# Gate and up products as seven Strassen products of halves, with the weight sums made by adding transfers

## The chip, the cores and the metric

The kernel runs on one core of one Trainium2 chip. The metric is the device time of one execution in microseconds (us). The engines are TensorE (PE, matrix products), VectorE (DVE), ScalarE (ACT), GpSimd (POOL) and SyncE (SP, which here only issues transfers); ACT and POOL issue transfers too, in order with their arithmetic. The 16 DMA engines are shared by all of them.

## The reference

One block on x of 512 rows and 1024 columns, all in float32:

```
proj  = rmsnorm(x) @ w_in
out_a = gated_delta_rule(conv(q, k, v), g, beta) -> norm, gate z -> @ w_o
out_b = silu(layernorm(conv31(glu))) @ w_pw2 + b
x  = x + (gate_a * out_a + gate_b * out_b) @ w_out
h2 = rmsnorm(x)
x  = x + (silu(h2 @ w_gate) * (h2 @ w_up)) @ w_down     # hidden width 2816
return rmsnorm(x) * norm_f_w
```

## The kernel before

A float32 product is made of three: weight and operand are each split into a high part in the matmul's format (`whi`, `hh`) and the rest (`wlo`, `hl`), and `split3` (L107 to L113) issues high x high, high x low and low x high. `unit` (L92 to L105) brings weights in: SP loads 128 x 1024 values into `raw`, ACT copies the high part (L102), DVE subtracts (L104). Each of the three has three buffers, so SP can run three units ahead.

The stages follow one another on PE: the input projection with the deltanet heads worked in between (to about 440 us), the gates, the eight column tiles of `wo` (490 to 532), the eight of `wpw` (532 to 575), `w_out` (`tok_mm`, to 621), then the channel mixer. In the wo stage the layernorm of the convolution branch is worked beside the products: ACT squares (L574), POOL sums them (L575), a root (L582), eight silu (L586), and then eight `yh` (L728) with their rests `yl` (L729), which are the operands of wpw. Behind `w_out` comes the second norm: squares on ACT (L794), POOL's `rms_half` (L796, L798), a scaling, transposes on PE and the split into `hh`, `hl` (L828).

The hidden width is 22 tiles of 128. For each tile f the gate and the up product have 8 k-tiles x 3 matmuls of 128 x 512; silu on ACT (L881), the product on DVE (L888). For f below 11 POOL also makes the sums of the down weights (`sums`, L860 to L868): one load, four additions, one store to `wsum` in DRAM. The down product is Winograd's form of Strassen: seven products of halves over 11 k-tiles, two at a time by `two`, the last one (p3) alone, with the final norm (`norm_f`, L911 to L922) running into the end.

The order on each engine is the order in which the scheduler puts the program's lines, by when their inputs come. `behind` and `issue_after` hold an instruction behind another one of its engine.

## Time and profile before

| what | value |
|---|---|
| median of 3 runs | 987.75 us (987.21 to 988.66) |
| profiled execution | 987.57 us |
| its span | 985.8 us |
| mean granted clock of PE | 0.994 |
| bytes moved by DMA | 138.50 MB |

The difference of 1.8 us between the profiled execution and its span lies around the program. In a row of a timeline the first number is the start and the second the duration in us; the bracket holds the idle time ahead of it and what ended it. In a row of a group, the number behind x is the count, then busy time and the mean of one in ns.

### The profile page before, as it was taken

Reading aid. Unit: us, or ns where it says so; the run is one execution under the profiler, and the core shown is the slowest. Engines: PE = TensorE matmul, PEld = TensorE weight load, DVE = VectorE, ACT = ScalarE, POOL = GpSimd, SP = SyncE. Lnnn points to the kernel's source line nnn. Section 1 sums busy time; section 2 is a strip of 40 time slices with the busy share of each in tenths; the row PEclk is TensorE's granted clock in tenths of the full one; section 3 lists DMA queues with packets and bytes.
Section 4 is the critical chain, followed back from the end, with each engine's and each line's share of the span. In section 5 each row is a group of like instructions: output and inputs, shape, how many; then the busy total and the mean of one; then the engine's idle time right before and its main releaser. Section 6 shows DMA issues by size and latency. Waiting matters only on the chain.

```text
span 985.8 us, 13439 instructions
## 1 busy us (share of the span) xinstructions
PE 955.7 (97%) x4775; PEld 785.7 (80%) x4775; DVE 669.8 (68%) x1044; ACT 513.6 (52%) x1062; POOL 255.1 (26%) x410
## 2 busy tenths in 40 slices
...
GB/s 317 88 119 120 120 91 41 127 68 98 77 65 88 65 87 69 97 124 144 272 137 137 146 115 65 166 192 246 186 242 206 203 211 184 92 168 196 160 207 86
DMA packets 48291, 138.50 MB, mean 140 GB/s; under 512 B 7472, under 2 KB 9424, under 8 KB 45408
## 3 DMA queue, kind: packets, MB, share of 16 engines
q1 hardware_dynamic: 44016, 112.36, 34.4%
q0 software_dynamic: 3488, 24.17, 6.9%
q10 hardware_dynamic: 720, 1.11, 0.3%
q8 instruction: 37, 0.61, 0.3%
...
## 4 chain that ended last, share of the span: by engine, by line
PE 84%; ACT 5%; DVE 4%; POOL 4%; issue 2%; DMA 1%; SPq 0%; POOLq 0%; ACTq 0%; DVEq 0%
PE mm L113 64%; PE w L113 11%; DVE wlo L104 1%; POOL Un L350 1%; ACT cp L355 1%; ACT Un L349 1%; PE st L477 1%; PE b L415 1%; PE b L421 1%; PE st L483 1%; POOL ytm L376 1%; PE st L489 1%; PE g L346 1%; DMA raw<-in_win_dram 1%; PE st L478 1%
## 5 line engine op out<-in xcount | busy, mean ns | idle before, releaser
L102 ACT ACTIVATE whi<-raw 128x1024 fp32r<-128x1024 f32 x167 | 176.1, 1057 | 327.1 <-PE mm L113 191.9
L113 PE MATMUL mm<-hh,whi 128*128 128x512 f32 x816 | 325.9, 400 | 0.0
L113 PE MATMUL mm<-hl,whi 128*128 128x512 f32 x816 | 321.9, 395 | 2.3 <-POOL hl L229 1.6
L113 PE MATMUL mm<-hh,wlo 128*128 128x512 f32 x816 | 322.3, 395 | 0.0
L104 DVE TENSOR_TENSOR wlo<-raw,whi 128x1024 fp32r<-128x1024 f32 x167 | 214.5, 1285 | 114.7 <-ACT whi L102 114.1
L545 DVE SCALAR_TENSOR_TENSOR cps<-c,c31w,cps 128x512 f32<-128x512 f32 x240 | 180.0, 750 | 4.9 <-ACT cps L543 1.0
L113 PEld LDWEIGHTS mm<-hl,whi 128*128 128x128 f32 x816 | 153.5, 188 | 33.0 <-POOL hl L229 2.9
L113 PEld LDWEIGHTS mm<-hh,wlo 128*128 128x128 f32 x816 | 153.4, 188 | 30.1
L113 PEld LDWEIGHTS mm<-hh,whi 128*128 128x128 f32 x816 | 153.5, 188 | 29.2 <-ACT hh L228 0.2
L888 DVE TENSOR_TENSOR fm<-mm,fsg 128x512 f32<-128x512 f32 x21 | 14.5, 692 | 67.0 <-PE mm L113 67.0
L300 DVE SCALAR_TENSOR_TENSOR acc<-mm,c4w,acc 128x509 f32<-128x509 f32 (+2 forms) x72 | 52.6, 738 | 1.5 <-ACT acc L297 1.2
L376 POOL TENSOR_TENSOR ytm<-U,y 128x60 f32<-128x60 f32 (+14 forms) x120 | 36.9, 307 | 60.6 <-DMA U<-sc 51.9
L113 PE MATMUL mm<-yh,whi 128*128 128x512 f32 x128 | 50.6, 396 | 0.0
L113 PE MATMUL mm<-yh,wlo 128*128 128x512 f32 x128 | 49.8, 389 | 0.0
L113 PE MATMUL mm<-yl,whi 128*128 128x512 f32 x128 | 49.8, 389 | 0.0
L113 PE MATMUL w<-whi,fh 128*128 128x512 f32 (+1 forms) x115 | 45.3, 395 | 2.8 <-ACT whi L102 2.8
L113 PE MATMUL w<-wlo,fh 128*128 128x512 f32 (+1 forms) x115 | 45.6, 397 | 2.4 <-DVE wlo L104 2.4
L113 PE MATMUL w<-whi,fl 128*128 128x512 f32 (+1 forms) x115 | 45.0, 393 | 0.0
L378 POOL TENSOR_TENSOR y<-y,ytm 128x60 f32<-128x60 f32 (+14 forms) x120 | 34.9, 291 | 9.4
L511 POOL TENSOR_TENSOR ss<-ss,half 128x4 f32<-128x4 f32 x8 | 8.1, 1014 | 109.5 <-DVE ss L509 109.5
L796 POOL TENSOR_SCALAR ss<-ss 128x1 f32<-128x1 f32 x17 | 5.7, 338 | 117.9 <-ACT sg L794 105.3
L864 POOL TENSOR_TENSOR wst<-wst 128x512 f32<-128x512 f32 x11 | 15.2, 1386 | 62.7 <-DMA wst<-in_wdn_dram 62.7
...
## 6 DMA issues: line engine op xcount, KB each, us to landing
raw<-in_win_dram SPq DMA_DIRECT2D x61, 512.0 KB, 3.3
raw<-in_wgu_dram SPq DMA_DIRECT2D x44, 512.0 KB, 3.4
...
A<-in_x_dram SPq DMA_DIRECT2D x8, 512.0 KB, 6.3
...
```

The lines of the kernel that those rows point to most:

```text
L102: marked(S.activation(hi[:, 0:n], raw[:, 0:n], AF.Copy), "unit")
L104: marked(V.tensor_tensor(out=lo[:, 0:n], in0=raw[:, 0:n], in1=hi[:, 0:n].bitcast(F32), op=ALU.subtract), "unit")
L113: marked(PE.matmul(ps, l, r, start=first and i == 0, stop=last and i == 2))
L300: marked(V.scalar_tensor_tensor(out=acc[:, s:], in0=ps[:, :T - s], scalar=c4w[:, j, k:k + 1], in1=acc[:, s:], op0=ALU.mult, op1=ALU.add))
L346: PE.matmul(ps[:, n, :], kT[:, n, :], kT[:, n, :], start=True, stop=True)
L349: S.activation(Un[:, n, :], ps[:, n, :], AF.Copy, scale=nb2[:, n:n + 1])
L350: G.tensor_tensor(out=Un, in0=Un, in1=DT, op=ALU.mult)
L376: G.tensor_tensor(out=tm[:, :, 0:w], in0=U[:, k, :, k + 1:], in1=y[:, :, k:k + 1].broadcast_to([P, NT, w]), op=ALU.mult)
L378: last[0] = G.tensor_tensor(out=y[:, :, k + 1:], in0=y[:, :, k + 1:], in1=tm[:, :, 0:w], op=ALU.add)
L545: V.scalar_tensor_tensor(out=acc, in0=c[:, k:k + T], scalar=c31w[:, i, k:k + 1], in1=acc, op0=ALU.mult, op1=ALU.add)
L864: G.tensor_tensor(out=b11, in0=b12, in1=b11, op=ALU.subtract)
L888: V.tensor_tensor(out=fm, in0=pu, in1=sg, op=ALU.mult)
```

## The change

The gate and up products of f = 2 to 21 are made together by `pair`: rows of a tile's weights (k 0 to 3, k 4 to 7) and columns of the operand (256 tokens each) are halved, and seven products of 4 k-tiles x 3 matmuls of 256 columns take the place of eight such blocks. f = 0 and 1 stay as they were. The operands' sums (`xb`, `T2`, `T3`, `T4`) are made once, on DVE and POOL. The weights' sums s1 to s4 (20 tiles of 128 x 512, 5.24 MB each) and those of the down product t1 to t4 (11 tiles, 2.88 MB each) are made in DRAM: `begin` copies one array (from ACT, four pieces), `plus` adds another to it by an accumulating transfer (from POOL, four pieces). POOL's `sums` goes. The gated values `fm` of all 22 tiles stay on chip, y1 goes to DRAM (`ysp`) after the second norm and comes back as `y2` in the first down product, and the final norm's lines are put in another order.

```diff
-    def unit(ap):
-        n = 1024
-        raw = wp.tile([P, 1024], F32, name="raw")
-        if isinstance(ap, tuple):
-            n = T * len(ap)
-            for i, p in enumerate(ap):
-                nc.sync.dma_start(raw[:, i * T:(i + 1) * T], p)
-        else:
-            nc.sync.dma_start(raw.rearrange("p (a c) -> p a c", a=2) if len(ap.shape) == 3 else raw, ap)
-        hi = wp.tile([P, 1024], F32R, name="whi")
-        marked(S.activation(hi[:, 0:n], raw[:, 0:n], AF.Copy), "unit")
-        lo = wp.tile([P, 1024], F32R, name="wlo")
-        marked(V.tensor_tensor(out=lo[:, 0:n], in0=raw[:, 0:n], in1=hi[:, 0:n].bitcast(F32), op=ALU.subtract), "unit")
+    loads = []
+    def unit(ap, pool=None):
+        aps = ap if isinstance(ap, tuple) else (ap,)
+        n = T * len(aps) if isinstance(ap, tuple) else 1024
+        raw, hi, lo = ((pool or wp).tile([P, n if pool else 1024], t, name=x)[:, 0:n]
+                       for t, x in ((F32, "raw"), (F32R, "whi"), (F32R, "wlo")))
+        for i, p in enumerate(aps):
+            loads.append(nc.sync.dma_start(raw[:, i * T:(i + 1) * T] if len(aps) > 1 else raw, p))
+        marked(S.activation(hi, raw, AF.Copy), "unit")
+        marked(V.tensor_tensor(out=lo, in0=raw, in1=hi.bitcast(F32), op=ALU.subtract), "unit")
         return hi, lo
...
+    FK, F0 = FF // 2, 2
+    sums = {n: dram.tile([FF - F0, P, T], F32, name=n, bufs=1) for n in ("s1", "s2", "s3", "s4")}
+    sums.update({n: dram.tile([FK, P, T], F32, name=n, bufs=1) for n in ("t1", "t2", "t3", "t4")})
+    gu = {n: a["wgu"][r * FF + F0:(r + 1) * FF][:, :, c * T:(c + 1) * T]
+          for n, r, c in (("A11", 0, 0), ("A12", 0, 1), ("A21", 1, 0), ("A22", 1, 1))}
+    gu.update({n: a["wdn"][:, :, c * T:(c + 1) * T] for n, c in (("B11", 0), ("B12", 1), ("B21", 2), ("B22", 3))})
+    src = lambda n: sums[n] if n in sums else gu[n]
+    def pieces(n):
+        f = sums[n].shape[0]
+        return [slice(i * f // 4, (i + 1) * f // 4) for i in range(4)]
+    def begin(n, m, ps=range(4)):
+        with behind(mybir.EngineType.Activation):
+            for p in ps:
+                nc.scalar.dma_start(sums[n][pieces(n)[p]], src(m)[pieces(n)[p]])
+    def plus(n, m, ps=range(4), behind_=None):
+        with tc.issue_after(behind_.ins) if behind_ else nullcontext():
+            for p in ps:
+                nc.gpsimd.dma_start(sums[n][pieces(n)[p]], src(m)[pieces(n)[p]], accum_op=ALU.add)
...
-                G.tensor_tensor(out=vacc, in0=vacc, in1=sq2, op=ALU.add)
+                last[0] = G.tensor_tensor(out=vacc, in0=vacc, in1=sq2, op=ALU.add)
...
+    plan = [(at + 15 * i, f, n, m, [i]) for at, f, n, m in ((100, begin, "s1", "A21"), (160, begin, "s3", "A11"))
+            for i in range(4)]
+    plan += [(at + 40 * i, f, n, m, [2 * i, 2 * i + 1]) for at, f, n, m in
+             ((165, plus, "s1", "A22"), (240, plus, "s3", "A21"), (260, begin, "s2", "s1"), (330, plus, "s2", "A11"))
+             for i in range(2)]
+    plan.sort(key=lambda p: p[0])
     while step() or chains:
+        while plan and plan[0][0] <= count[0]:
+            _, f, *w = plan.pop(0)
+            f(*w, *([last[0]] if f is plus else []))
...
         col_tile(ps, a["wo"][j], oh, ol)
+        if j == 3:
+            begin("s4", "s2")
+        if j in (5, 7):
+            begin(*(("t1", "B11") if j == 5 else ("t3", "B22")))
         ma = mp.tile([P, T], F32, name="ma", bufs=KD + 1)
...
+        if j in (0, 3, 5):
+            plus(*(("s4", "A12") if j == 0 else ("t1", "B12") if j == 3 else ("t3", "B12")), behind_=last[0])
...
         if hf:
+            nc.scalar.dma_start(ysp[n], y1[:, n, :])
...
-    def sums(k):
-        r = fp.tile([P, 4, T], F32, name="wst", bufs=1)
-        nc.gpsimd.dma_start(r, a["wdn"][k].rearrange("p (i c) -> p i c", i=4))
-        b11, b12, b21, b22 = (r[:, i, :] for i in range(4))
-        G.tensor_tensor(out=b11, in0=b12, in1=b11, op=ALU.subtract)
-        G.tensor_tensor(out=b12, in0=b22, in1=b12, op=ALU.subtract)
-        G.tensor_tensor(out=b22, in0=b22, in1=b11, op=ALU.subtract)
-        G.tensor_tensor(out=b21, in0=b22, in1=b21, op=ALU.subtract)
-        nc.gpsimd.dma_start(wsum[k], r)
...
-        if f < FK:
-            sums(f)
-            set1.append(xset())
-            hi, lo = (t[:, t1] for t in set1[f])
-            xsplit(hi, lo, fm[:, t1])
...
+    def operands(f):
+        if f < FK:
+            set1.append(xset())
+            hi, lo = (t[:, t1] for t in set1[f])
+            xsplit(hi, lo, fms[f][:, t1])
+            return
+        b, fm = fms[f - FK], fms[f]
+        s1 = fq.tile([P, TH], F32, name="s1")
+        tt(s1, b[:, t2], fm[:, t2], ALU.subtract)
+        hi, lo = (t[:, t2] for t in set1[f - FK])
+        xsplit(hi, lo, s1)
+        tt(b[:, t2], b[:, t1], b[:, t2], ALU.subtract, G)
+        last[0] = tt(b[:, t1], s1, b[:, t1], ALU.subtract, G)
...
+    kl, kh = slice(0, KH), slice(KH, KD)
+    xb = []
+    for i, (ks, ts, eng) in enumerate(((kl, t1, V), (kl, t2, V), (kh, t2, V), (kh, t1, G))):
+        xb.append(fx.tile([P, KH, TH], F32, name="xb%d" % i))
+        tt(xb[i], hh[:, ks, ts].bitcast(F32), hl[:, ks, ts].bitcast(F32), ALU.add, eng)
+    b11, b12, b22, b21 = xb
+    tt(b11, b11, b12, ALU.subtract)
+    tt(b12, b22, b12, ALU.subtract, G)
+    tt(b22, b22, b11, ALU.add)
+    tt(b21, b22, b21, ALU.subtract)
+    T2, T3, T4 = ([fq.tile([P, KH, TH], F32R, name="%s%d" % (n, i)) for n in ("th", "tl")] for i in range(3))
+    xsplit(*T4, b21)
+    S.activation(T2[0], b22, AF.Copy, scale=-1.0)
+    V.scalar_tensor_tensor(out=T2[1], in0=b22, scalar=-1.0, in1=T2[0].bitcast(F32), op0=ALU.mult, op1=ALU.subtract)
+    xsplit(*T3, b12)
+    B11, B21, B22 = ([t[:, ks, ts] for t in (hh, hl)] for ks, ts in ((kl, t1), (kh, t1), (kh, t2)))
+    T1 = [t[:, kl, t2] for t in (hh, hl)]
+    def hprod(ps, w, i, x):
+        for k in range(KH):
+            c = slice(i * T + k * P, i * T + k * P + P)
+            split3(ps, (w[0][:, c], w[1][:, c]), x[0][:, k, :], x[1][:, k, :], k == 0, k == KH - 1)
...
+    def pair(f):
+        z = [bank() for _ in range(4)] if f % 2 == 0 else [bank(), bank2(), bank2(), bank2()]
+        s = lambda n: sums[n][f - F0]
+        w = unit(a["wgu"][f])
+        w46 = unit((a["wgu"][FF + f][:, T:], s("s2")))
+        hprod(z[0][:, t1], w, 0, B11)
+        hprod(z[1][:, t1], w, 1, B21)
+        hprod(z[2][:, t1], w46, 0, T4)
+        w37 = unit((s("s4"), s("s3")))
+        hprod(z[0][:, t2], w46, 1, T2)
+        cw = fq.tile([P, T], F32, name="cw", bufs=2)
+        S.copy(out=cw[:, t1], in_=z[0][:, t1])
+        u = fq.tile([P, TH], F32, name="cu")
+        tt(u, cw[:, t1], z[0][:, t2], ALU.add)
+        hprod(z[1][:, t2], w37, 0, B22)
+        w5 = unit((s("s1"),), we)
+        hprod(z[3][:, t1], w37, 1, T3)
+        v = fq.tile([P, TH], F32, name="cv2")
+        tt(v, u, z[3][:, t1], ALU.add)
+        if f == F0:
+            xsplit(*T1, b11)
+        hprod(z[2][:, t2], w5, 0, T1)
+        tt(cw[:, t2], u, z[2][:, t2], ALU.add)
+        fm = hidden()
+        tt(fm.rearrange("p (i t) -> p i t", i=2), z[2].rearrange("p (i t) -> p i t", i=2),
+           v.rearrange("p (a t) -> p a t", a=1).broadcast_to([P, 2, TH]), ALU.add)
+        tt(cw, cw, z[1], ALU.add)
+        S.activation(cw, cw, AF.Silu)
+        V.scalar_tensor_tensor(out=fm, in0=fm, scalar=-1.0, in1=cw, op0=ALU.mult, op1=ALU.mult)
+    ff = None
+    for f in range(F0, FF):
+        pair(f)
+        if f == 3:
+            begin("t2", "t3")
+        if f == FK + 2:
+            plus("t2", "B11", behind_=last[0])
+        if f == FK + 5:
+            begin("t4", "t2")
+        if f == FK + 8:
+            plus("t4", "B21", behind_=last[0])
+        if ff is None:
+            fxs.close()
+            ff = ctx.enter_context(tc.tile_pool(name="ff", bufs=FK))
+            for i in range(F0):
+                operands(i)
+        operands(f)
...
+    def first_half(n):
+        squares(0, n, c1)
+        G.tensor_tensor(out=o0[n], in0=y2[:, n, c1], in1=nfw[:, c1], op=ALU.mult)
+    def out(n):
+        S.activation(o0[n], o0[n], AF.Copy, scale=ss3[:, 3, n:n + 1])
+        nc.scalar.dma_start(a["out"][n][:, c1], o0[n])
+        scaled_out(n, c2, nc.sync)
...
+        also = list(also)
         for k in range(FK):
             w = unit(weights(k))
+            if also:
+                with tc.issue_after(loads[-1].ins):
+                    nc.sync.dma_start(*also.pop(0))
             for i in range(2):
                 prods(w, i, xs[k], i, banks[2 * i:2 * i + 2], k == 0, k == FK - 1)
-            then(k)
...
+    def set_3(k):
+        set3.append(xset())
+        xsplit(*set3[k], fms[FK + k])
+        tt(fms[k][:, t1], fms[FK + k][:, t1], fms[k][:, t1], ALU.add, G)
...
-        add(2 + n, c1, p4[n], op=ALU.subtract)
-        norm_f(0, 2 + n, c1)
-        norm_f(1, 2 + n, c2)
-        add(n, c1, p2[n])
-        norm_f(0, n, c1)
+    two(lambda k: (wd(k, 2), wt(k, 4)), set3, p2 + p4, set_4)
...
+        if k < 2:
+            add(2 + k, c1, p4[k])
+            squares(0, 2 + k, c1)
+            squares(1, 2 + k, c2, True)
+        elif k < 4:
+            add(k - 2, c1, p2[k - 2])
+            for cs, eng in ((c1, nc.scalar), (c2, nc.sync)):
+                scaled_out(k, cs, eng)
+            first_half(k - 2)
...
     add(0, c2, p3[0])
-    norm_f(1, 0, c2)
+    squares(1, 0, c2, True)
     add(1, c2, p3[1])
     for c, b in ((0, bank), (256, bank2)):
         ps = b()[:, c:c + 256]
@@ -1013,7 +1153,10 @@
             part(k, 1, ps, c, 256, k == K0, k == FK - 1)
         cs = slice(T + c, T + c + 256)
         add(1, cs, ps)
-        norm_f(4 if c else 1, 1, cs)
+        squares(4 if c else 1, 1, cs, c)
+        if not c:
+            out(0)
+    out(1)
```

Here a transfer signals one of eight counters when it has landed (DMAHW0 to 7 for SP and ACT, DMASW0 to 7 for POOL), and a transfer that gets a counter in use waits for the one before it on that counter. Numbers behind a tile's name tell buffers apart.

ACT, from the layernorm's table to the first operand of wpw. Before:

```order
L582 ACT_TABLE_LOAD
L582 ACTIVATE pa<-mm,epsc 128x512
L102 ACTIVATE whi<-raw 128x1024
L586 ACT_TABLE_LOAD
L586 ACTIVATE cv<-cv,vec 128x512 x8
L728 ACTIVATE yh<-cv 128x512 x8
L102 ACTIVATE whi<-raw 128x1024 x3
```

Now, with what each waits for (the seven silu before `cv_108` left out). s4 has been issued ahead of this, after the third, fifth and eighth square, on DMAHW6, 5, 6 and 7:

```order
L158 DMA t1_128<-in_wdn_dram 384x512 [waits DMAHW5_49]
L615 ACT_TABLE_LOAD
...
L615 ACTIVATE cv_108<-cv_108,vec_77 128x512 [waits DVE_49]
L158 DMA t1_128<-in_wdn_dram 384x512 [waits DMAHW6_49]
L158 DMA t1_128<-in_wdn_dram 384x512 [waits DMAHW7_49]
L103 ACTIVATE whi_5347<-raw_5346 128x1024 [waits DMAHW1_49]
L103 ACTIVATE whi_5382<-raw_5381 128x1024 [waits DMAHW1_49,Activation_49]
L158 DMA t3_130<-in_wdn_dram 256x512 [waits DMAHW0_49]
L158 DMA t3_130<-in_wdn_dram 384x512 [waits DMAHW5_49]
L158 DMA t3_130<-in_wdn_dram 384x512 [waits DMAHW6_49]
L158 DMA t3_130<-in_wdn_dram 384x512 [waits DMAHW7_49]
L767 ACTIVATE yh_5419<-cv_101 128x512 [waits PE_49,Activation_49]
```

Between the silu and `yh` (L767, before L728) stand six copies and two `whi`. t1's last two pieces hold for s4's third and fourth, t3's pieces for t1's.

POOL, from the last sum of squares to the second norm. Before:

```order
L575 TENSOR_TENSOR sacc_5113<-sacc_5113,acc4_5141 128x512
L796 TENSOR_SCALAR ss2_5734<-ss2_5734 128x1 x5
L798 TENSOR_TENSOR ss2_5734<-ss2_5734,half_81 128x1
L796 TENSOR_SCALAR ss2_5734<-ss2_5734 128x1
L798 TENSOR_TENSOR ss2_5734<-ss2_5734,half_81 128x1
```

Now, twelve accumulating transfers in one row (five of them left out):

```order
L604 TENSOR_TENSOR sacc_5145<-sacc_5145,acc4_5173 128x512 [waits Activation_49,Pool_49]
L163 DMA s4_127<-in_wgu_dram 640x512 [waits DMAHW6_49,DMASW6_49]
...
L163 DMA s4_127<-in_wgu_dram 640x512 [waits DMAHW7_49,DMASW1_49]
L163 DMA t1_128<-in_wdn_dram 256x512 [waits DMAHW0_49,DMASW2_49]
...
L163 DMA t1_128<-in_wdn_dram 384x512 [waits DMAHW7_49,DMASW5_49]
L163 DMA t3_130<-in_wdn_dram 256x512 [waits DMAHW0_49,DMASW6_49]
...
L163 DMA t3_130<-in_wdn_dram 384x512 [waits DMAHW7_49,DMASW1_49]
L843 TENSOR_SCALAR ss2_5794<-ss2_5794 128x1 [waits Activation_49] x4
```

The second norm's step (L843, before L796) now stands behind all of s4, t1 and t3; t3's issues wait for counters that s4's additions hold.

ACT, at the end of the transposes behind the second norm. Before:

```order
L828 ACTIVATE hh<-mm 128x4x128
L794 ACTIVATE sg,ss_5734<-A 128x512
L828 ACTIVATE hh<-mm 128x4x128 x3
L102 ACTIVATE whi<-raw 128x1024
L881 ACTIVATE fsg<-w 128x512
```

Now:

```order
L876 ACTIVATE hh_91<-mm_6127 128x4x128 [waits PE_49]
L103 ACTIVATE whi_6457<-raw_6456 128x512 [waits DMAHW2_49,DMAHW6_49,DMAHW0_49,DMAHW7_49,DVE_49,Activation_49]
L103 ACTIVATE whi_6601<-raw_6600 128x512 [waits DMAHW7_49]
L158 DMA t2_129<-t3_130 16x8192 [waits DMASW6_49]
L876 ACTIVATE hh_91<-mm_6196 128x4x128 [waits PE_49]
L876 ACTIVATE hh_91<-mm_6203 128x4x128 [waits PE_49]
```

The copy that begins t2 has come between the `hh` copies (L876, before L828); it waits on DMASW6 for the addition to t3's first piece.

125 lines of the change are left out of this document (61 added, 64 removed).

## The prediction

> **What bounds the kernel now.** I read the engines' busy time and the chain that ended last first, then stretches of each stage, then single rows.
>
> ```profile
> PE 955.7 (97%) x4775; PEld 785.7 (80%) x4775; DVE 669.8 (68%) x1044; ACT 513.6 (52%) x1062; POOL 255.1 (26%) x410
> PE 84%; ACT 5%; DVE 4%; POOL 4%; issue 2%; DMA 1%; SPq 0%; POOLq 0%; ACTq 0%; DVEq 0%
> ```
>
> TensorE (PE) is busy 97% of the span and is 84% of the chain. So a change gains by what it takes off PE, or by closing a hole in PE, and it loses where it makes PE wait. The stretch of the gate and up products:
>
> ```profile
> 700.00:800.00 100.00, 100.00 (x443) 82.81 (x442) 41.82 (x52) 29.13 (x39) 37.11 (x32) 1.00 0.61 218
> ```
>
> Columns: busy us of PE, PEld, DVE, ACT, POOL, then granted clock, DMA share, GB/s. PE has no hole and the full clock; nothing but fewer PE cycles helps there. One hole is near the end:
>
> ```profile
> 963.43 0.39 PE L113 MATMUL mm<-wlo,fh 128*128 128x512 f32 x1
> 966.66 0.50 PE L113 MATMUL w<-whi,fh 128*128 128x512 f32 x1 [2.84 <-ACT whi L102]
> ...
> 968.74 0.79 PE L113 MATMUL w<-wlo,fh 128*128 128x512 f32 x1 [1.35 <-DVE wlo L104]
> 969.33 0.63 PE L113 MATMUL w<-whi,fh 128*128 128x512 f32 x1
> 969.75 0.63 PE L113 MATMUL w<-whi,fl 128*128 128x512 f32 x1
> ...
> 974.24 0.41 PE L113 MATMUL w<-wlo,fh 128*128 128x512 f32 x1
> 974.48 0.39 PE L113 MATMUL w<-whi,fh 128*128 128x512 f32 x1
> 963.57 0.72 ACT L918 ACTIVATE o<-o,ss 128x512 f32<-128x512 f32 x1 [4.85 <-POOL ss L798]
> 964.32 0.37 ACTq L921 DMA_DIRECT2D out_dram<-o  x1
> 965.56 1.04 ACT L102 ACTIVATE whi<-raw 128x1024 fp32r<-128x1024 f32 x1
> 970.00:975.00 5.00, 5.00 (x18) 4.19 (x18) 1.02 (x2) 0.00 (x0) 0.00 (x0) 0.57 0.01 2
> ```
>
> ACT sits 4.85 us on POOL's norm work (L798); the weight copy `whi` queued behind it comes at 965.56, and PE waits 2.84 us and then 1.35 us. After the hole the granted clock falls to 0.57: matmuls of 512 columns start 0.42 us apart until 974.24, and 0.23 behind it.
>
> **The change, part by part.**
>
> *Fewer PE cycles.* A gate/up pair was 2 tiles x 8 k x 3 = 48 matmuls of 512 columns; twenty of the 22 pairs become 7 products x 4 k x 3 = 84 of 256 columns. Both sizes run in the trace:
>
> ```profile
> 528.75 0.39 PE L113 MATMUL mm<-yl,whi 128*128 128x512 f32 x1
> ...
> 531.92 0.39 PE L113 MATMUL mm<-yh,whi 128*128 128x512 f32 x1
> ...
> 533.97 0.39 PE L113 MATMUL mm<-yh,whi 128*128 128x512 f32 x1
> 632.04 0.28 PE L113 MATMUL w<-hl,whi 128*128 128x256 f32 x1
> ...
> 635.64 0.28 PE L113 MATMUL w<-hh,wlo 128*128 128x256 f32 x1
> ```
>
> The durations overlap, so the pace is the distance of starts: 23 steps from 528.75 to 533.97, 0.227 us; 30 steps from 632.04 to 635.64, 0.120 us. 20 x 48 x 0.227 = 217.9 us become 20 x 84 x 0.120 = 201.6 us: **-16.3 us**.
>
> *VectorE (DVE) must keep up.* A pair now splits 3.5 weight units instead of 2 and adds PSUM halves:
>
> ```profile
> L104 DVE TENSOR_TENSOR wlo<-raw,whi 128x1024 fp32r<-128x1024 f32 x39 | 53.3, 1368 | 56.9 <-ACT whi L102 56.9
> L888 DVE TENSOR_TENSOR fm<-mm,fsg 128x512 f32<-128x512 f32 x19 | 13.1, 692 | 60.3 <-PE mm L113 60.3
> L902 DVE TENSOR_TENSOR fm<-s,fm 128x256 f32<-128x256 f32 x9 | 4.8, 534 | 0.3
> L898 DVE TENSOR_TENSOR s<-fm 128x256 f32<-128x256 f32 x9 | 5.6, 620 | 0.3
> ```
>
> 3.5 x 1.37 + 3 x 0.69 + 5 x 0.53 to 0.62 is 9.5 to 10.0 us of DVE in 84 x 0.120 = 10.08 us of PE. It fits barely, and these rows were taken beside POOL's weight sums (37 us of 100), which go away. The operand sums and splits before the first pair are ten DVE passes of the `wlo` size, 13.7 us, and two on POOL; with four weight splits DVE has 19.2 us to do in the 17.4 us of PE from 632 to the first product that needs them (3.6 for the rest of f=0, 10.9 for f=1, 2.9 for two products). I take **+2 us** for both (bounds 0 and 8). The loads fit: 1.79 MB a pair in 10.1 us is 178 GB/s, under the 218 above.
>
> *The tail.* The change puts squares, scaling and stores of the norm behind the last weight copies on ACT. Hole and slow clock should go: 2.84 + 1.35 us of waiting, half of the 4.9 us from 969.33 to 974.24, and 0.36 at the matmul before (0.59 instead of 0.23): 4.2 + 2.8. I take **-7.0 us** (bounds -4.2, if some slow clock stays, and -7.0).
>
> *The deltanet stage.* Copies and adding transfers of s1, s3, s2 (15.7 MB copied, as much added) run in a stage with a free queue, at the price of ACT issues and of loads behind them:
>
> ```profile
> 300.00:400.00 100.00, 97.57 (x574) 80.57 (x574) 75.97 (x148) 62.23 (x171) 25.64 (x68) 1.00 0.26 82
> ```
>
> I take **+1.5 us** (bounds 0 and 5); the cover is the 74% of the queue that is free there.
>
> *The start of the wpw stage.* This is the term that decides. ACT issues the copies of s4, t1 and t3 (5.24, 2.88 and 2.88 MB) in the wo stage, in order with its arithmetic. In the order of instructions, t1's last two pieces wait until s4's third and fourth have landed, and t3's four pieces until t1's four have landed; all of this stands ahead of the first `yh` (L728 before). So `yh` now needs 8.12 MB copied.
>
> ```profile
> 503.30 0.63 ACT L574 ACTIVATE acc<-cv 128x512 f32<-128x512 f32 x1 [1.11 <-POOL sacc L575]
> 523.40 5.76 ACT L586 ACTIVATE cv<-cv,vec 128x512 f32<-128x512 f32 x8
> 529.07 4.26 ACT L728 ACTIVATE yh<-cv 128x512 fp32r<-128x512 f32 x8
> 529.71 2.50 DVE L729 TENSOR_TENSOR yl<-cv,yh 128x512 fp32r<-128x512 f32 x4 [1.20 <-ACT yh L728]
> 505.00:530.00 25.00, 25.00 (x110) 20.21 (x109) 21.22 (x22) 16.41 (x21) 9.19 (x5) 1.00 0.39 118
> q1 hardware_dynamic: 44016, 112.36, 34.4%
> q0 software_dynamic: 3488, 24.17, 6.9%
> raw<-in_wgu_dram SPq DMA_DIRECT2D x44, 512.0 KB, 3.4
> ```
>
> Before, `yh` starts at 529.07, its first `yl` is ready at 529.71 + 0.62 = 530.3, and PE's first wpw matmul comes at 531.92: a slack of 1.6 us. The first s4 piece is issued after the third square, at 504. No copy inside DRAM is in this trace; the nearest rows are loads: 112.36 MB in 34.4% of 985.8 us, 331 GB/s while busy (software queue: 355).
>
> Lower bound, copies always there in time: only six issues of 0.37 us and two `whi` of 1.06 us stand ahead of `yh`: 4.3 - 1.6 = 2.7 us. Middle: until 532 the copies get the 61% that the weight loads leave, 202 GB/s x 28 us = 5.65 MB; then PE stands, the loads stop with full buffers, and 2.47 MB go at 331 in 7.5 us, to 539.4; 1.8 us to land (a 512 KB load takes 3.4, of which 1.6 is bytes) and 0.4 for an issue give 541.6, so `yh` is 12.5 late and PE 10.9. A wait that long also brings the slow clock of the tail, 2.75 us. Upper: the adding transfers of s4 run at once and take half: by 532 2.83 MB, the other 5.29 MB at 165 GB/s in 32 us, `yh` at 566.2: 35.5 + 2.75 = 38.3 us. I take the middle, **+13.7 us**, since a plain transfer is the nearest row and the adding ones start later.
>
> *Behind it.* POOL's norm2 step stands behind twelve adding transfers, ACT's last `hh` copies behind a copy that waits for t3's first sum.
>
> ```profile
> 608.61 0.28 POOL L796 TENSOR_SCALAR ss<-ss 128x1 f32<-128x1 f32 x1 [8.77 <-ACT sg L794]
> 628.76 1.09 ACT L828 ACTIVATE hh<-mm 128x512 fp32r<-128x512 f32 x2 [4.39 <-PE mm L826]
> ```
>
> The second is tighter: 5.24 + 2.88 + 0.52 = 8.65 MB added between 512 and 640 (628.76 and the delay) need 68 GB/s. Later t2's sum (2.88 MB) has the three pairs from f=13 to f=16, 30 us, before ACT's copies of t4 wait for it: 95 GB/s. I take 0, since both queues of the rows do over three times that; without that rate it is rival B.
>
> **Sum** against the profiled execution's 987.57 us (the median of the runs, 987.75, is 0.02% above; span 985.8 and 1.8 around it): 987.57 - 16.3 - 7.0 + 2 + 1.5 + 13.7 = **981.5 us**.
>
> The Trainium skill, DMA: Bandwidth & Descriptors (Latency and other measured facts), gives 214 GB/s as the full rate of plain copies between HBM tensors, well under the 331 of these loads; no run here shows one yet. By that page 61% of 214 until 532 and then 214 would bring `yh` at 555, 27 us instead of 13.7, and the sum would be 995: slower than before. The Trainium skill, Collectives: The Full Stack (The bandwidth ceiling), says that a transfer which adds is slower because it reads two sources, and that a reduction moves at half the rate of a copy; by that the adding transfers would run near half of 331, still above the 95 that they need.
>
> **The rivals.**
>
> A, *the copies are slower: wpw starts 20 to 40 us late.* Break-even is a term of 19.8 us (987.57 - 16.3 - 7 + 3.5 + 19.8); less 2.75 for the clock, `yh` is 18.7 late, at 547.8, and the copies must average 8.12 MB / (545.6 - 504) = 195 GB/s. Below that the kernel is slower; with halves for the adding transfers 981.5 - 13.7 + 38.3 = **1006 us**. For it: the adding transfers overlap in time, and a copy inside DRAM reads and writes there. Against it: before 532 the loads leave 61%.
>
> B, *adding is slow.* At 60 GB/s the 8.65 MB take 144 us, to 656, 16 us behind the last `hh` copies, and t2's sum 48 instead of 30: **about 1000 us** with the first alone and the clock, 1018 with both. For it: nothing in the trace has such a transfer. Against it: 95 GB/s is under a third of what the queue does.
>
> C, *all hidden.* The copies keep 330 GB/s from 504 on and land in time: 2.7 in place of 13.7, no slow clock: **970.5 us**.
>
> D, *the pairs are no cheaper.* If a 256-column matmul took 0.130 us (0.010 more), or DVE set the pace at 10.9 us a pair, the 16.3 would be gone: **997.8 us**. The 0.120 stands over 30 matmuls in a row, but with weights already split.
>
> **How the numbers follow.** A measurement of this kernel can tell about 0.2%, 2 us. The forecast with 974 to 985.6 has 0.40; C 0.16; the slice between the forecast and A, 985.6 to 989.6, 0.11; A beyond that 0.20; B 0.08; D 0.05. So faster 0.56, within 0.2% 0.11, slower 0.33. The likeliest case's own range is 974 to 986; for 8 in 10 it reaches into C (without the 3.5 for DVE and the deltanet stage: 967) and into A as far as 1004.
>
> **What would show it.** Right: in the gate/up stretch PE without holes and 84 matmuls each 10.1 us; no wait for `whi` at L103 in the last 25 us; one wait of PE of about 11 us for `yh` (L767) after wo, and behind it a clock under 1.00; ACT's copies of s4 and t1 landing by about 540. Wrong: a wait over 20 us there (A), PE waiting at `hh` or at ACT's squares of norm2 (B), `wlo` as releaser of PE all through the pairs (D), waits for `U` or `raw` before 490 (the 1.5 was too small).

## The result, and the profile after

The changed kernel takes **1164.39 us** in the median of 4 runs (1159.46 to 1166.23), against 988.2 for the kernel before beside it: a ratio of 1.177 (95% interval 1.173 to 1.182). The prediction was 981.5 us with a range to 1004, so it was wrong in sign and 160 us short of the result at the end of its range. Of the runs below, one of the two executions of `held_copies` (1156.64 us at a granted clock of 0.754, against 0.989 in the other) is left out.

The stages in the profiled executions, each from the start of its first matmul on PE (us):

| stage | before | after | difference |
|---|---|---|---|
| projection, deltanet, gates (up to wo) | 486.6 | 585.7 | +99.1 |
| wo and wpw | 88.9 | 135.9 | +47.0 |
| w_out and the second norm | 46.2 | 51.6 | +5.5 |
| gate and up products | 242.4 | 234.7 | -7.7 |
| down products and final norm, to PE's end | 114.0 | 146.3 | +32.3 |

More than half of the loss stands in a stage to which the prediction gave 1.5 us, and a fifth in the down products, from which it took 7.0. From the page of the kernel after: busy tenths of PE and its granted clock over 40 slices, the queues, and the landing times of the new transfers (KB each, median us).

```profile
PE   7999866988995989999695579988999999987697
PEclk9999979878997979999687889989999999989999
DMA  8234241467865637844169998354655696487454
q0 software_dynamic: 16704, 33.61, 16.4%
...
s<-in_wgu_dram POOLq DMA_DIRECT2D x16, 1280.0 KB, 21.2
...
s<-in_wgu_dram ACTq DMA_DIRECT2D x8, 1280.0 KB, 6.6
s<-s ACTq DMA_DIRECT2D x8, 1280.0 KB, 8.4
t<-in_wdn_dram POOLq DMA_DIRECT2D x12, 768.0 KB, 18.4
```

PE has holes from the first eighth of the span to the last. The clock is low in most of them or just behind (6 to 8 tenths), so that such a hole is paid twice; in the holes of the last four slices it is not. An adding transfer of 1.31 MB lands 21.2 us after its issue in the median, where a copy of the same size takes 6.6 us. That is not the rate of one addition: they are issued two or four at a time and land one behind another. Of the pair that is issued at 249.9 and 250.7 us the first takes 10.5 us, 124 GB/s, and the second 21.7 (after, `s`, POOL, 249.5 to 251.5 us):

```profile
DMA to landing us min/median/max: 10.5/16.1/21.7
```

Ahead of wo the DMA engines are not full; 0.62 is their share in this window of the same kernel (PE, PEld, DVE, ACT and POOL busy, granted clock, DMA share, GB/s), in which PE's clock is 0.84. In the slices of wo, wpw and w_out the DMA row of the page has up to 9 tenths.

```profile
200.00:300.00 100.00, 84.77 (x444) 68.92 (x445) 42.32 (x98) 60.15 (x171) 37.35 (x75) 0.84 0.62 168
```

The waits of PE by releaser, after (total, count, longest):

```profile
PE mm L113 <- ACT whi L103: 38.8, 6, 11.7
PE mm L113 <- DVE wlo L104: 16.4, 4, 14.1
PE st L517 <- ACT w L514: 14.4, 7, 9.4
PE w L113 <- ACT whi L103: 13.5, 10, 3.4
PE g L342 <- ACT vT L332: 10.5, 1, 10.5
```

PE's own releasers are ACT and DVE, not DMA. The first large wait that the kernel before does not have, of 10.5 us, is a wait for `vT`, and it begins at 142 us, before any adding transfer has run. Rows of the engines around it, after (timelines of DVE, ACT and PE):

```profile
131.33 12.61 DVE L574 SCALAR_TENSOR_TENSOR cps<-c,c31w,cps 128x512 f32<-128x512 f32 x16
...
144.02 0.13 DVE L367 TENSOR_SCALAR ss<-ss 128x4 f32<-128x4 f32 x1
144.60 1.14 ACT L378 ACTIVATE Un<-g,ss 128x128 f32<-128x128 f32 x4 [11.09 <-DVE ss L370]
...
151.88 0.63 ACT L332 ACTIVATE vT<-acc 128x512 f32<-128x512 f32 x1
152.57 0.47 PE L342 MATMUL g<-cst,vT 128*128 128x128 f32 x1 [10.50 <-ACT vT L332]
```

DVE runs 16 steps of the 31-tap convolution in a row, 12.6 us, ahead of a 0.13 us operation that the deltanet head needs. ACT stands 11 us for it, and PE 10.5 us for ACT. No transfer is in this chain: what has changed there is the **order** of the instructions on DVE. The prediction had no step for that.

### The profile page after: what moved, and what is told of

Same layout as the page of the kernel before. It is cut to its first block, busy times and chain, and to the rows that moved or that the text cites. A ratio compares the mean times of both kernels' runs of the same rounds, so it can differ in the third digit from the quotient of the medians.

```text
span 1161.3 us, 15383 instructions
## 1 busy us (share of the span) xinstructions
PE 1003.8 (86%) x5495; PEld 844.6 (73%) x5495; DVE 757.4 (65%) x1163; ACT 557.8 (48%) x1127; POOL 254.1 (22%) x409
## 5 line engine op out<-in xcount | busy, mean ns | idle before, releaser
L104 DVE TENSOR_TENSOR wlo<-raw,whi 128x1024 fp32r<-128x1024 f32 (+1 forms) x207 | 248.6, 1206 | 121.0 <-ACT whi L103 115.4
L103 ACT ACTIVATE whi<-raw 128x1024 fp32r<-128x1024 f32 (+1 forms) x207 | 207.6, 1013 | 234.5 <-PE mm L113 107.7
L113 PE MATMUL mm<-hh,whi 128*128 128x512 f32 (+1 forms) x616 | 238.3, 387 | 16.2 <-ACT whi L103 16.2
L113 PE MATMUL mm<-hh,wlo 128*128 128x512 f32 (+1 forms) x616 | 234.0, 380 | 2.2 <-DVE wlo L104 2.2
L113 PE MATMUL mm<-hl,whi 128*128 128x512 f32 (+1 forms) x616 | 233.8, 380 | 2.3 <-POOL hl L258 1.6
L113 PEld LDWEIGHTS mm<-hh,whi 128*128 128x128 f32 x616 | 118.9, 193 | 35.6 <-ACT whi L103 18.3
L113 PEld LDWEIGHTS mm<-hh,wlo 128*128 128x128 f32 x616 | 118.1, 192 | 23.7 <-DVE wlo L104 4.3
L113 PEld LDWEIGHTS mm<-hl,whi 128*128 128x128 f32 x616 | 118.8, 193 | 21.2 <-POOL hl L258 2.9
L113 PE MATMUL w<-hh,whi 128*128 128x256 f32 x232 | 65.9, 286 | 1.2 <-ACT hh L903 0.9
L113 PE MATMUL w<-hl,whi 128*128 128x256 f32 x232 | 65.7, 284 | 0.9 <-DVE hl L877 0.9
L113 PE MATMUL w<-hh,wlo 128*128 128x256 f32 x232 | 65.7, 283 | 0.3 <-DVE wlo L104 0.3
L329 DVE SCALAR_TENSOR_TENSOR acc<-mm,c4w,acc 128x511 f32<-128x511 f32 (+2 forms) x72 | 52.9, 741 | 7.2 <-ACT acc L326 6.8
## 6 DMA issues: line engine op xcount, KB each, us to landing
s<-in_wgu_dram POOLq DMA_DIRECT2D x16, 1280.0 KB, 21.2
```

Source lines behind the costliest of these rows:

```text
L103: marked(S.activation(hi, raw, AF.Copy), "unit")
L104: marked(V.tensor_tensor(out=lo, in0=raw, in1=hi.bitcast(F32), op=ALU.subtract), "unit")
L113: marked(PE.matmul(ps, l, r, start=first and i == 0, stop=last and i == 2))
L329: marked(V.scalar_tensor_tensor(out=acc[:, s:], in0=ps[:, :T - s], scalar=c4w[:, j, k:k + 1], in1=acc[:, s:], op0=ALU.mult, op1=ALU.add))
```

## Experiment 1: the same program without the large transfers

Two kernels keep the change's arithmetic and its own scheduling. `plain_weights` drops all copies and additions of weight sums, and each unit reads a block of plain weights of the same size in place of a sum (so the channel mixer no longer computes the reference's values). `small_transfers` issues all of them, but each with 2 of the 128 rows of a tile, 1/64 of the bytes, and reads plain blocks too. The edits in short:

```diff
 plain_weights
-    src = lambda n: sums[n] if n in sums else gu[n]
+    src = lambda n: gu[plain.get(n, n)]     # plain: s1 -> A21, t1 -> B12, ...
-    begin(...), plus(...)
 small_transfers
-  nc.scalar.dma_start(sums[n][pieces(n)[p]], src(m)[pieces(n)[p]])
+  nc.scalar.dma_start(sums[n][pieces(n)[p]][:, 0:2], src(m)[pieces(n)[p]][:, 0:2])
   (the adding transfer likewise)
```

> The change without any of its weight sums: no copy and no adding transfer is issued, and where the pairs and the down product would read a sum they read a plain block of the weights, of the same size (the values of the channel mixer are then not the reference's; everything else is computed). It prices the pairs, the operand sums and the tail alone. By the prediction's terms: 987.6 - 16.3 (PE) - 7.0 (tail) + 2 (DVE) = 966 us. If the pairs themselves are the loss (VectorE sets their pace, 10.9 us a pair or more), it stays at 985 or above; then the sums are not what costs.

> The change with its own, not held, order, but each copy and addition cut to 2 of 128 rows of every block (1/64 of the bytes; plain blocks are read in the place of the sums, so the channel mixer's values are not the reference's). Number, place and waits of the transfers stay. If the size that the scheduler counts is what spoils the order, this is near plain_weights: 970 to 985 us. If 32 transfers of any size spoil it, it is 1050 us or more.

`plain_weights` takes **970.12 us** (ratio 0.9805, 0.9777 to 0.9833), `small_transfers` 972.45 (0.9839, 0.9803 to 0.9876). So neither the pairs, nor the number of the transfers, nor their issues cost anything that shows. What is left is the bytes of the transfers, or that loads wait for the sums: in both kernels no load reads one.

Gate and up in `plain_weights` take 227.5 us instead of 242.4. From its windows:

```profile
680.00:705.00 25.00, 25.00 (x211) 25.00 (x210) 19.60 (x30) 11.68 (x17) 0.00 (x0) 1.00 0.57 180
705.00:730.00 25.00, 25.00 (x211) 25.00 (x210) 17.93 (x27) 12.64 (x18) 0.00 (x0) 1.00 0.58 187
...
865.00:870.00 5.00, 2.25 (x10) 1.56 (x9) 1.00 (x2) 1.43 (x2) 0.74 (x1) 1.00 0.99 349
870.00:875.00 5.00, 5.00 (x16) 3.99 (x15) 4.01 (x4) 2.88 (x4) 0.73 (x1) 0.66 0.59 211
...
950.00:962.00 12.00, 11.91 (x67) 10.30 (x65) 9.08 (x12) 5.74 (x12) 7.57 (x9) 1.00 0.30 111
```

PE is full in the pairs, 211 matmuls in 25 us, 0.118 us each, with DVE at 0.72 to 0.78. In the last 12 us the old hole in the tail is gone, with the clock at 1.00. But the down products start with a new hole: at 865 the DMA share is 0.99, as the four reloads of y1 (512 KB each) come beside the weights, and PE waits.

```profile
869.67 0.50 PE L113 MATMUL w<-whi,fh 128*128 128x512 f32 x1 [2.75 <-ACT whi L103]
```

## Experiment 2: the order and the transfers, one at a time

The order on the engines can be held. The kernel is built twice: the first build notes the order that the scheduler gives each engine, and the second adds an edge from each instruction to the next of its engine, so that the order stays whatever transfers it issues. (Line numbers are 2 to 12 higher in these kernels than in the kernel after.) In short:

```diff
+    first = traced_program(MODEL, ("note", state))   # which sums this build makes
+    nc = traced_program(LIVE, ("hold", state))       # which sums the kernel makes
+    for engine, ks in state["order"].items():
+        for x, y in zip(ks, ks[1:]):
+            tc.add_manual_dep(traced[y], traced[x].name, NoSync, reason="hold_order")
 order_only:      MODEL = all sums, LIVE = none (plain blocks are read)
 transfers_only:  MODEL = none,     LIVE = all  (the change's full result)
```

> As plain_weights (no sum is made, plain blocks are read), but every engine's instructions are held in exactly the order that the changed kernel has, by issue-order edges alone. So it has the change's order without its transfers. Theory 1, transfers: the added 65 MB and the waits for them cost the 176 us; then this runs like plain_weights, 966 us, the stretch up to the first wo matmul 487 us. Theory 2, order: the scheduler, which counts the added transfers in its own time model, puts the engines' work in another order, and that order is what is slow; then this is 1080 us or more, with about 70 to 99 us of the loss ahead of the first wo matmul (at 560 to 586 us), and ScalarE waiting behind VectorE's convolution steps as in the changed kernel.

> The mirror image: all copies and adding transfers of the change, with the sums read as in the change (full result), but every engine's other instructions held in the order of plain_weights, in which the deltanet stage is the order of the kernel before. Theory 1, transfers: 1140 us or more, as the change. Theory 2, order: the deltanet stage ends within 10 us of before (first wo matmul by 497 us), and what is left is the wait for the copies at the start of wpw and the slow additions behind it, 990 to 1040 us in all.

| kernel | us | up to wo | wo, wpw | w_out | gate, up | down |
|---|---|---|---|---|---|---|
| plain_weights | 970.12 | 487.9 | 88.9 | 46.2 | 227.5 | 111.5 |
| order_only | 1127.4 | 576.7 | 116.0 | 51.5 | 234.0 | 139.1 |
| transfers_only | 1013.45 | 492.2 | 112.6 | 46.2 | 237.5 | 116.8 |
| the change | 1164.39 | 585.7 | 135.9 | 51.6 | 234.7 | 146.3 |

The ratios to before are 1.140 (1.136 to 1.143) and 1.024 (1.021 to 1.027). Against `plain_weights` the **order alone costs 157.3 us**, with not one byte of the sums moved. The **transfers alone cost 43.3 us**. Together that is 200.6 us; the change has 194.3. Holding an order is not what costs: `deltanet_sums` below is held too, moves 31 MB more and ends 5.6 us behind `plain_weights`. The page of `order_only` has the same waits as the kernel after, by the same releasers:

```profile
127.51 12.61 DVE L586 SCALAR_TENSOR_TENSOR cps<-c,c31w,cps 128x512 f32<-128x512 f32 x16
148.75 0.47 PE L354 MATMUL g<-cst,vT 128*128 128x128 f32 x1 [10.51 <-ACT vT L344]
PE mm L115 <- ACT whi L105: 29.6, 7, 11.7
PE st L529 <- ACT w L526: 12.8, 6, 9.4
PE g L354 <- ACT vT L344: 10.5, 1, 10.5
```

In `plain_weights` the convolution steps stand singly and in threes between the head's operations, and the same transposition has no wait at all:

```profile
129.07 0.74 DVE L584 SCALAR_TENSOR_TENSOR cps<-c,c31w,cps 128x512 f32<-128x512 f32 x1
129.72 0.15 DVE L377 TENSOR_SCALAR ss<-ss 128x4 f32<-128x4 f32 x1
...
132.46 2.32 DVE L584 SCALAR_TENSOR_TENSOR cps<-c,c31w,cps 128x512 f32<-128x512 f32 x3
136.96 0.60 PE L352 MATMUL g<-cst,vT 128*128 128x128 f32 x4
```

How waits become 89 us before wo is seen in the windows with the sums of that stage, of `plain_weights` and then of `order_only`:

```profile
sum 488.00, PE 471.50 PEld 384.62 DVE 396.58 ACT 325.55 POOL 131.98; mean PE 94.30 PEld 76.92 DVE 79.32 ACT 65.11 POOL 26.40
```

```profile
200.00:300.00 100.00, 93.41 (x480) 76.71 (x480) 39.24 (x94) 61.59 (x176) 30.53 (x71) 0.84 0.22 70
...
sum 577.00, PE 506.79 PEld 410.84 DVE 399.55 ACT 328.51 POOL 139.06; mean PE 84.47 PEld 68.47 DVE 66.59 ACT 54.75 POOL 23.18
```

DVE and ACT do the same work (397 and 400 us, 326 and 329). PE stands 70 us instead of 16.5, and the work that it does takes 507 us instead of 472; the clock is 0.84 in such a stretch, where `plain_weights` has 1.00. So of 89 us some 54 are holes and 35 slower work between them.

In the down products the order does another thing. In the second of them PE waits at every unit, in the kernel after:

```profile
1061.73 0.50 PE L113 MATMUL w<-whi,fh 128*128 128x512 f32 x1 [0.92 <-ACT whi L103]
1065.67 0.50 PE L113 MATMUL w<-whi,fh 128*128 128x512 f32 x1 [0.92 <-ACT whi L103]
```

A unit takes 3.94 us instead of 2.72. `order_only` has the same step of 3.94. In PE's order the second halves of the last two units of the first product stand behind eight units of the second. So those two keep their buffers until then, and of three buffers one is left for the second product. That is read from the order of the matmuls; no run tests it apart.

## Experiment 3: how little changes the order

`order_by_copies` and `order_by_additions` hold the order that the scheduler gives to a program with the copies alone, or with the additions alone, and run without either (plain blocks are read). `one_copy` is the kernel before with a single copy of 1.31 MB that nobody reads, scheduled as it comes. Its edit:

```diff
+    spare = dram.tile([5, P, T], F32, name="spare", bufs=1)
+        if one and count[0] >= 100:
+            one.pop()
+            with behind(mybir.EngineType.Activation):
+                nc.scalar.dma_start(spare, a["wgu"][FF + 2:FF + 7][:, :, 0:T])
```

> As order_only (plain blocks read, no transfer of the sums issued, the channel mixer's values not the reference's), but held in the order that the scheduler makes of a program with all the copies and none of the additions. If the copies alone make it rearrange the engines (they stand in its model ahead of the weight loads), the loss is most of order_only's 157 us over plain_weights: 1080 us or more, with the first wo matmul after 540 us. If it is the additions, it is within 10 us of plain_weights' 970.

> The counterpart: the order that the scheduler makes of a program with all the additions and none of the copies, again without any of these transfers on the chip. If the copies are the cause, it stays within 15 us of 970; if the additions are, it is 1080 us or more. If both are slow, any large transfer in its model is enough, and the loss is that of a fragile order, not of one kind of transfer.

> The kernel before with one transfer more: at step 100 of the deltanet stage ScalarE issues a copy of five weight blocks (1.31 MB, inside DRAM) that nobody reads. Result as the reference. On the chip such a copy takes 7 us of a queue that is a quarter full there, so if only the transfer counts it costs nothing: 988 us. If the order is fragile (the scheduler sets other instructions ahead from this copy on, on all five engines), it loses tens of us in the deltanet stage: 1010 us or more, with the first wo matmul after 505 us.

They take 1095.24 (ratio 1.108, 1.103 to 1.112), 1182.53 (1.196, 1.191 to 1.200) and 996.1 us (1.008, 1.006 to 1.011). One unread copy costs 8 us, far less than the tens that were expected of it. It costs them by the same 16 convolution steps in a row and the same wait as the change, and in the window of 136 to 150 us the DMA engines move 0.14 MB:

```profile
127.34 12.61 DVE L545 SCALAR_TENSOR_TENSOR cps<-c,c31w,cps 128x512 f32<-128x512 f32 x16
...
148.58 0.48 PE L313 MATMUL g<-cst,vT 128*128 128x128 f32 x1 [10.50 <-ACT vT L303]
```

Each kind of transfer gives a bad order by itself, and their prices do not add up: the additions' order is worse alone than the change's. In `small_transfers` all 64 transfers are there and the time is good. So the number of the transfers alone does not spoil the scheduler's order. That it answers to their **size**, counted as time, is likely but not shown: `small_transfers` has no load that reads a sum, and the order of the change comes from a program in which they do. `one_copy` alone has the size without a reader, and it gives 8 us, against the 157.

## Experiment 4: what the transfers cost where the order is held

`deltanet_sums` makes s1, s3 and s2 alone (the rest is read plain). `held_copies` is `transfers_only` without the additions. `held_all_early` makes all sums before wo. `held_spread` makes s4 around wo and spreads the down sums over wpw and the pairs, a piece at a time. `held_late_sums` puts the s4 additions behind the layernorm's sums, reloads y1 at every second unit and starts t2 and t4 one or two tiles earlier. All hold the order of `plain_weights`, and the last three make and read all sums. In short:

```diff
 held_all_early: in the plan of the deltanet stage
+  (20, begin t1) (56, begin t3) (110, plus t1) (140, plus t3) (210, begin t2) (285, plus t2)
+  (385, begin t4) (410, plus t4) (440, begin s4); wo: plus s4 at j = 1, 3
 held_spread:    s4 copied at 440; plus s4 at j = 1, 3 of wo; t1, t3 copied singly in wpw;
                 plus t1 behind them, t3 (in twos), t2, t4 singly in the pairs
 held_late_sums: plus s4 at j = 4, 6 of wo instead of 1, 3
-            if also:
+            if also and k % 2:
```

> Only the sums s1, s3 and s2 are made (copies and additions in the deltanet stage, 31 MB); the other sums are left out and plain blocks read in their place, so the channel mixer's values are not the reference's. Order held as in plain_weights. It splits transfers_only: by theory 1 the first wo matmul comes at 580 us, by theory 2 at 487 to 497 us, and the end is 966 us plus that delay. An addition of one piece (1.31 MB) took 21 us in the changed kernel, 62 GB/s; if that is its own rate and not that of a crowded queue, it is 18 to 21 us here too.

> transfers_only without its additions: the order held, all copies as in the change, no adding transfer; the sums then hold plain blocks, so the channel mixer's values are not the reference's. It tells the prediction's term for the start of wpw apart: the middle was 10.9 us of waiting, reckoned without the additions, the upper bound 35.5 us with them at half the rate; transfers_only showed 20.9. If copies alone set the wait by bytes, it is 9 to 13 us here. If the additions were what made it longer, it falls below 11; if it stays at 20, the additions did not matter and the copies run slower than a load.

> A full version (result as the reference): the order of plain_weights held, and all copies and additions moved ahead of the wo stage but s4's additions, two pieces at a time: t1 and t3 copied from step 20, added from step 110, t2 and t4 and s4 begun between steps 210 and 460. transfers_only lost 21 us at the start of wpw and 15 us to bursts in the last pairs and the down product; with the copies gone from there only the deltanet stage pays: 4.3 us for 31 MB there, in proportion about 10 us for the 65 MB. Expected 970 + 10 = 980 us (974 to 990). If the additions starve the deltanet's own loads as the queue fills, the deltanet stage is 20 us longer and it is no faster than before.

> The other full version (result as the reference): order held, s1, s3, s2 as in the change, s4 begun ahead of wo, and one piece of t1, t3, t2, t4 at a time from the second wpw column on to the last pairs, never four in a row. The wait for yh (20.9 us in transfers_only) goes, and the 7 us hole at the burst of four copies in the last pairs goes. Expected 970 + 4.3 + 3 = 977 us (973 to 985). If it is the amount moved and not the burst that makes PE wait there, the pairs take 237 us as in transfers_only instead of 228, and it ends at 985 or more.

> held_spread with two mends (result as the reference): s4's additions come on GpSimd behind the layernorm's sums, where they made PE wait 7 us, and the four reloads of y1 in the first down product are put at every second k instead of in a row (plain_weights has a hole of 2.75 us with the slow clock behind it there). Expected: plain_weights 970 + 4 for the deltanet stage + 0 to 3 in the pairs - 4 for the reloads, 973 us (969 to 980). If the reloads were not the cause of that hole it is 977.

| kernel | us | ratio | up to wo | wo, wpw | w_out | gate, up | down |
|---|---|---|---|---|---|---|---|
| deltanet_sums | 975.72 | 0.986 (0.983 to 0.989) | 492.4 | 88.9 | 46.2 | 227.5 | 111.7 |
| held_copies | 982.08 | | 488.0 | 99.9 | 46.2 | 227.5 | 111.2 |
| held_all_early | 1006.5 | 1.018 (1.015 to 1.021) | 510.0 | 100.2 | 46.2 | 227.5 | 111.2 |
| held_spread | 992.39 | 1.004 (1.002 to 1.006) | 491.1 | 99.5 | 46.2 | 230.6 | 115.0 |
| held_late_sums | 989.02 | 1.002 (0.999 to 1.004) | 490.1 | 88.9 | 52.8 | 234.7 | 111.3 |

(The stages are those of the profiled execution, and for `held_copies` the time is too.) The wait at the start of wpw that the prediction priced is there. `transfers_only`, then `held_copies`:

```profile
558.52 0.79 PE L115 MATMUL mm<-yh,whi 128*128 128x512 f32 x1 [20.88 <-ACT yh L779]
```

```profile
542.10 0.79 PE L115 MATMUL mm<-yh,whi 128*128 128x512 f32 x1 [8.14 <-ACT yh L779]
```

It is 8.1 us with copies alone and 20.9 with the additions beside them. In the change itself ACT loses 18.3 us at the same place:

```profile
670.87 4.27 ACT L767 ACTIVATE yh<-cv 128x512 fp32r<-128x512 f32 x8 [18.28 <-DMA t<-in_wdn_dram]
```

All three versions with everything moved miss their expectations by 15 us or more: `held_spread` and `held_late_sums` end near the time before, `held_all_early` 18 us above it. They lose at different places: `held_all_early` ahead of wo and in wpw, `held_spread` mostly where POOL's additions stand ahead of the layernorm's sums, `held_late_sums` in w_out and the pairs. It looked as if the bytes had their price wherever they lie.

## Experiment 5: a price of places or of traffic

Three more versions hold the order and move transfers only. They followed from comparing, matmul by matmul, the start on PE with that of `plain_weights`: the lag of a held version is flat for hundreds of us and rises at a few points. In short:

```diff
 held_placed: s2 and s4 wholly before wo
-  (165, plus s1) (240, plus s3) (260, begin s2) (330, plus s2) (440, begin s4)
+  (165, plus s1) (225, begin s2) (240, plus s2) (280, plus s3) (300, begin s4) (330, plus s4)
 held_late_heads: nothing started from 190 to 285 us; t2 and t4 some 60 us earlier
-  (100, begin s1) (160, begin s3) (165, plus s1) (225, begin s2)
+  (60, begin s1) (120, begin s3) (110 and 240, plus s1) (255, begin s2)
   ...
 held_last_move: on top of that
-  (110 and 240, plus s1) (255, begin s2)
+  (110, plus s1) (280, begin s2)
```

> The whole change, all sums made and read, order of plain_weights held, transfers put elsewhere than in held_late_sums: s2 and s4 are wholly made inside the deltanet stage (s2's copies at 275 and 310 us, its additions from 308, s4's copies from 363, its additions from 400 to 447), so that no addition stands on POOL near the layernorm sums or beside w_out for s4; t1 is copied in wpw and added there and in w_out, t3, t2 and t4 in the pairs, one piece in flight, as in held_spread; the reloads of y1 are spread as in held_late_sums. If the price left with the order held is one of place (a few loads that stand on the chain of the heads before 290, yh, the eight units of w_out), the losses are 2 to 5 us before wo, none in wo, wpw and w_out, 3 in the pairs, none in the down products: 970.1 + 5 to 8, 975 to 979 us, and faster than before. If it is the traffic as such (65 MB more through the same engines, wherever they lie), it ends where the other spread versions do, 987 to 993 us.

> held_placed lost nothing between 300 and 780 us, and its losses against plain_weights stand at three places: 5.9 us near 240 and 8.6 near 285, where s3's copies (208 to 234) and s2's (268, 271) meet the heads' loads of DT and U, and 6 to 8 from 790 on, where t2's and t4's additions end beside the first down product. Here the copies of s1 and s3 are issued before about 190 us, nothing is issued from there to 300 but one pair of additions, s1's second half, s2, s3 and s4 follow from 300 to 490, t3 is finished before w_out ends, and t2 and t4 are made some 60 us earlier in the pairs. If the price is one of place, less than 3 us are left before 300 and 2 to 4 behind 780: 970.1 + 3 to 7, 973 to 977 us, faster than before. If it is the traffic, the waits come back at other instructions and it ends at 985 to 993 us again.

> As held_late_heads, with two moves. That run was level with plain_weights until 310 us and then lost 10 us at one place, 312 to 330, where s1's second half is added (285) and s2's first three copies start (291, 292, 314) beside the last loads of U; behind that it lost 1 us in 650. Here all of s1 is added from 164 on and s2's copies start at about 314. If place is what counts the 10 us at 312 to 330 go, at the risk of 2 to 4 us at the heads' loads near 185: 970.1 + 1 to 5, 971 to 976 us. If it is the traffic, the 8 to 10 us come back at another place: 980 to 985.

| kernel | us | ratio | up to wo | wo, wpw | w_out | gate, up | down |
|---|---|---|---|---|---|---|---|
| held_placed | 989.19 | 1.001 (1.000 to 1.003) | 505.0 | 88.9 | 46.2 | 229.8 | 117.1 |
| held_late_heads | 982.63 | 0.996 (0.993 to 0.998) | 498.4 | 88.9 | 46.2 | 230.1 | 109.3 |
| held_last_move | 982.73 | 0.994 (0.992 to 0.996) | 498.1 | 88.9 | 46.2 | 229.5 | 111.0 |

(The profiled execution of `held_placed`, with its stages, took 996.0 us, 7 more than the median.) The last two, with the change's full result, are **faster than before**, by 0.4 and 0.6%. That is little beside their scatter: the executions of `held_late_heads` go from 978.2 to 990.8 us, those of the kernel before beside it from 986.7 to 991.4. `held_placed` was level with `plain_weights` from 300 to 780 us but for a constant lag, though most of the sums are made there, and lost 14 us at 240 and 285 and 8 behind 780; `held_late_heads` was level up to 310 and lost 10 us from there to 330; `held_last_move` lost 8 us at 230 and 3 us at most in all the 700 behind it. The losses ahead of wo stand at a head's small transfers, in `held_placed` at the load of `DT` too, in the other two at the reload of `U`, the triangle that goes to DRAM as `sc` and comes back in eight loads of 64 KB. POOL waits for it, in `plain_weights`, in `held_late_heads` and in `held_last_move` (the row of `held_late_heads` names a copy that landed 0.2 us behind the last reload):

```profile
194.97 1.25 POOL L415 TENSOR_TENSOR ytm<-U,y 128x60 f32<-128x60 f32 x1 [8.70 <-DMA U<-sc]
...
316.64 0.29 POOL L415 TENSOR_TENSOR ytm<-U,y 128x60 f32<-128x60 f32 x1 [9.55 <-DMA U<-sc]
```

```profile
328.50 0.29 POOL L417 TENSOR_TENSOR ytm<-U,y 128x60 f32<-128x60 f32 x1 [21.14 <-DMA s<-s]
```

```profile
211.95 0.29 POOL L417 TENSOR_TENSOR ytm<-U,y 128x60 f32<-128x60 f32 x1 [20.03 <-DMA U<-sc]
229.36 0.80 PE L518 MATMUL st<-S,kT 128*128 128x128 f32 x2 [6.68 <-ACT o L539]
190.00:212.00 22.00, 22.00 (x136) 18.27 (x135) 18.47 (x38) 13.93 (x34) 1.35 (x2) 1.00 1.04 253
192.89 16.16 SPq L404 DMA_DIRECT2D U<-sc  x8
```

A wait of 9 us becomes 20 where additions and copies are in flight, and the head's chain, which PE needs some 17 us later, is late with it. In the window of 190 to 212 us the DMA share is 1.04: the engines are full, at only 253 GB/s. SP takes 16.2 us to issue the eight loads. In `plain_weights` it is 5:

```profile
187.84 4.96 SPq L402 DMA_DIRECT2D U<-sc  x8
```

The slow part of the 16.2 us is not the reload's own bytes. What SP waits for in `held_last_move` from 190 to 212 us is a transfer of a sum:

```profile
SPq L404 <- DMA s<-in_wgu_dram: 12.8, 2, 11.4
```

The fifth reload got the counter on which ACT had issued a copy of s3 at 178.6 us. Beside four additions that copy took 28.8 us, to 207.34, and SP issued the reload at 207.35. The last three reloads, on other counters, landed 3.1 to 3.6 us after their issue. So here it was a shared counter that passed the slowness of a background copy on to the head. In `held_late_heads` it was not: there the store of `sc` took 7.0 us instead of 2.4, and the reload behind it was slow itself.

Neither theory is left whole. Traffic as such costs little: between 330 and 700 us, where s2, s3, s4, t1 and most of t3 are made, the last two versions lose about 3 us. But the 10 us did not go with the last move. 8 of them came back at the reload of `U` 100 us earlier, and the time, 982.7, is the one that the theory of traffic expected. What is shown is where the loss sits: at a head's store and reload that meet additions and copies. POOL issues the additions at points of the program that stand some 20 to 30 us ahead of the reloads, and a group of them is in flight for 20 to 45. Whether a schedule that keeps every reload clear, or one in which no copy shares a counter with a reload, would come near 975 was not tried.

## Why the prediction was wrong, point by point

**The step that failed** is the one that is not in the sum: the work of the stages ahead of wo, and of the down products, was taken with the order of before. "The deltanet stage. Copies and adding transfers of s1, s3, s2 [...] run in a stage with a free queue" prices the transfers as load on a queue, 1.5 us; the stage took 99.1 us more. The price of the transfers alone was inside the bounds of 0 and 5: 4.5 us with the order held (`deltanet_sums`). The order alone takes 88.8 us more there (`order_only` against `plain_weights`). In the down products, where -7.0 was forecast and +32.3 came, it takes 27.6. Nothing in the sum says that the instructions of all five engines stand in another order from the first copy on. The order was read at three places only, all from the layernorm to the end of the second norm, where it had moved as the prediction says; the rest was argued from the trace of before, which is the trace of another order. This alone is 157 of the 194 us that the change lies above `plain_weights`, and no rival had it.

**Pairs, -16.3 + 2 us: right.** 227.5 instead of 242.4 us is -14.9; a matmul of 256 columns takes 0.118 us. Rival D falls. DVE is busy 7.1 to 7.8 us in a pair, less than the 9.5 to 10.0 that were reckoned. (The loads of a pair are 1.84 MB and not 1.79, which changes nothing.)

**Tail, -7.0 us: half.** The waits for `whi` in the tail are gone, as foreseen. The reloads of y1 made a hole of 2.75 us with a slow clock at the start of the down products, and only 2.5 us were left of 7. With the reloads spread and t2 and t4 early the stage takes 109.3 in `held_late_heads`, -4.7, but 111.0 in `held_last_move`, which has the same edits there.

**Start of wpw, +13.7 us (2.7 to 38.3): the mechanism right, the size between the ends.** With the order held PE waits 20.9 us for `yh`, and wo and wpw take 23.7 us more. Without the additions it waits 8.1 and they take 11.0 more. The middle, built from loads alone, gave 10.9 for the wait: it is near the copies, and the additions more than double it. The prediction took the additions to start later. s4's four were issued 2 us behind t1's copies (`transfers_only`, ACT and POOL):

```profile
516.47 3.04 ACTq L168 DMA_DIRECT2D t<-in_wdn_dram  x4
518.36 4.47 POOL L175 DMA_DIRECT2D s<-in_wgu_dram  x4
```

**Behind it, 0 us: wrong.** In `transfers_only` the gate and up products take 10.0 us more than in `plain_weights` and the down products 5.3. Rival B had t2 and t4 as the place, but not this wait. t2's four additions took 33.4 us from the first issue to the last landing, near the 30 that they had. But beside them, and then beside t4's copies, issued three in one row, the pairs' weights land late: a load issued at 800.9 us takes 12.1 us, where those of `plain_weights` take 2.6 to 4.2. ACT waits for them and PE for ACT (`transfers_only`):

```profile
815.88 1.76 ACTq L168 DMA_DIRECT2D t<-t  x3
828.63 1.06 ACT L105 ACTIVATE whi<-raw 128x1024 fp32r<-128x1024 f32 x1 [7.28 <-DMA raw<-s]
829.74 0.44 PE L115 MATMUL w<-hh,whi 128*128 128x256 f32 x1 [4.44 <-ACT whi L105]
```

For the transfers alone, with the order held, rival A comes nearest: 1006 us for 1013. In part that is luck, as it put 38.3 us at the start of wpw, where 23.7 are, and nothing in the pairs and the down products. As to the copies, the Trainium skill, DMA: Bandwidth & Descriptors (Latency and other measured facts), gives 214 GB/s for copies between HBM tensors, and 1.31 MB in 6.6 us is 199 GB/s with the latency in it, which agrees. The 995 us that the prediction worked out from that page for the wait at `yh` are nearer to the held version than its own 981.5, but by luck: they reckon copies alone, for which 27 us were 11.0. As to the additions, the Trainium skill, Collectives: The Full Stack (The bandwidth ceiling), has a reduction at half the rate of a copy. Here the first piece of each of the five groups of additions ahead of wo landed in 10.5 to 12.6 us (the kernel after), 104 to 125 GB/s, a little over half of a copy's 199, which agrees.

**Still open:** by which rule the scheduler turns the transfers into another order (their size, or the loads that wait for them), and which of the engines' orders carries most of the 157 us, since all five were held together.
